# New duration estimates and a charge for array-mode changes in the list scheduler of a hybrid attention / RWKV-7 / SwiGLU block

## Chip, core and metric

The kernel runs on one core of a Trainium2 chip. The metric is device time in microseconds (us) of one execution; lower is better. Engines are named as the profile names them: PE (TensorE matmul), PEld (TensorE weight load), DVE (VectorE), ACT (ScalarE), POOL (GpSimd), SP (SyncE, which issues the DMAs).

## What is computed

One encoder block on x of 1024 x 1024 float32:

```python
h = rms_norm(x, norm_mix_pre);  proj = h @ w_in
# attention, 8 heads of 64: for query block i, over keys s < t
z = q @ k.T * 64**-0.5
log_fail = where(strict, log_sigmoid(-z), 0)
after = cumsum(log_fail, reverse=True) - log_fail        # stick breaking
o_sb = where(strict, exp(log_sigmoid(z) + after), 0) @ v
# RWKV-7, 8 heads of 64, a scan over 1024 positions
state = state * w_t + (state @ -kk_t) (kk_t * a_t)' + v_t k_t';  y_t = state @ r_t
merged = gates[:D] * (o_sb @ w_sb_out) + gates[D:] * (o_rw @ w_rw_out)
x = x + rms_norm(merged @ w_o, norm_mix_post);  h = rms_norm(x, norm_ffn_pre)
x = x + rms_norm((silu(h @ w_ffn_gate) * (h @ w_ffn_up)) @ w_ffn_down, norm_ffn_post)
```

## The kernel before

The program is written as plain Python that *records* operations (`Block.record`), and a list scheduler (`Block.schedule`) then orders them for each engine; `Block.issue` emits that order, so every instruction carries one line, L528, and the tiles' names tell them apart. All engines run their own order strictly in sequence and wait for each other by semaphores.

**What sets the order.** `cost` (line 112) gives each recorded operation an estimated duration in ns. `LATENCY` and `MARGIN` give the time from the end of one operation to the earliest start of a dependent one on another engine. `schedule` (line 381) keeps, per engine, a time from which it is free, a heap of operations that are ready by then and a heap of those that become ready later. It always advances the engine that can act first and takes the ready operation with the lowest priority number: position in the program, plus offsets (`filler()` adds 10 million, the RWKV chain subtracts 1000, the triangular inverse 300). So filler products fill an engine only while, by the estimates, nothing urgent is ready. `run` (line 448) fixes start and end; on TensorE it adds the part of a weight load that the last product doesn't cover. `choose` (line 479) prefers, after a TensorE operation estimated under 70 ns, another one under 70 ns. `grant` and `Places` hand out SBUF and PSUM buffers in the same pass, so a changed order also changes which buffer a tile gets. PSUM has 8 banks in four classes of two: d, e, c, y. Operations recorded under `together()` form a bundle: TensorE issues its products one after another with nothing between.

**Wide products.** Most TensorE work is float32 split into a high and a low float32r part: every projection is three products per 128 contraction rows (`mm3`), each with 128 x 128 weights and 512 columns. These are called wides below; in the first half of the kernel they write PSUM class d and read `big_h`.

**Stages.** About 0 to 100 us: input norm, transposes, LoRA. About 100 to 550 us: RWKV, four pairs of heads, two halves of 512 positions each, so 8 units. For each unit `rw_elementwise` prepares the operands, `rw_inverse` inverts unit triangular 32 x 32 blocks on DVE (31 rounds of a TENSOR_TENSOR with a strided operand, tiles `q<-b_nl,q`, and a TENSOR_REDUCE) followed by bundles of 32 x 32 and 64 x 64 products, and `rw_chain` (line 985) walks 8 chunks of 64 positions in sequence. One step of the chain: TensorE `px` (c<-sv,nx), then DVE copies one half of px to `xv` and ACT the other, then TensorE `ps` (c<-xv,bkt), then two DVE SCALAR_TENSOR_TENSOR write the next state `sv`. The projections of the next pair and the gate projections are the filler. About 550 to 800 us: attention, `head` (line 1124), 4 pairs of heads, per pair a stretch of 68.2 us with the same order in the first three. Per query block: score products z (PSUM class e; the masked diagonal gets a 128 x 128 bfloat16 product), ACT sigmoid to `nb`, a DVE TENSOR_TENSOR_SCAN along up to 1024 keys in place in `nb`, TensorE transposes of `nb` into PSUM class c, ACT and DVE split these into `wt` (high, low), and TensorE multiplies by v into class y. About 800 to 960 us: merge of the two branches and output projection. From about 960 us: FFN with a seven-product Strassen-like scheme.

**Array modes.** A float32 product with 64 or 32 contraction rows or output columns uses only a part of the 128 x 128 array. Such narrow products (bundles in `rw_elementwise`, `rw_inverse` and `rw_chain`) stand between full-array products.

Of the kernel before, what the change touches and what calls it, by code (L numbers as in the profile page):

```python
# [7 lines left out]
F32R = mybir.dt.float32r  # L8
# [7 lines left out]
P = 128  # L16
# [16 lines left out]
CH = 64  # L33
# [41 lines left out]
def is_ap(x):  # L75
    return hasattr(x, "tensor") and hasattr(x, "offset") and hasattr(x, "ap")


def count(shape):
    n = 1  # L80
    for d in shape:
        n *= d
    return n
# [25 lines left out]
    return [(key, p0, p1, f, f + span) for f in starts]  # L109


def cost(engine, method, kw, in_psum):

    out = kw.get("out", kw.get("ap"))
    if out is None:
        return 1283.0
    n = count(out.shape[1:])
    if engine == "tensor":
        if method == "transpose":
            return max(out.shape[0], n) / 1.2  # L120
        m, full = count(kw["lhsT"].shape[1:]), kw["lhsT"].dtype == F32
        if out.shape[0] <= CH and n <= CH:
            return 65.0 if out.shape[0] == CH else 20.0
        return 2 * max(m, n) / 1.2 if full else max(m / 1.2, n / 2.4)
    psum = any(is_ap(v) and k not in OUTS and in_psum(v) for k, v in kw.items())
    if engine == "vector":
        if method == "tensor_copy" and not psum:
            return 60 + 0.52 * n
        if method == "tensor_reduce":
            n = count(kw["in_"].shape[1:])  # L130
            return 64 + 1.042 * n
        if method == "scalar_tensor_tensor":
            return max(196, 68 + (1.16 if psum else 1.1) * n)
        return 68 + 1.042 * n
    if engine == "scalar":
        extra = "accum_out" in kw or any(is_ap(kw.get(k)) for k in ("scale", "bias"))
        return 55 + 0.833 * n + (0 if psum else 40) + (90 if extra else 0)
    if engine == "gpsimd":
        if method == "memset":
            return 40.0  # L140
        if method == "tensor_copy":
            return 120 + 3.4 * n
        if method == "tensor_scalar":
            return 320 + 2.4 * n
        return 150 + 2.1 * n
    size = 4 * count(out.shape)
    return max(450.0, size / 360.0)
# [79 lines left out]
def wait(e, to):  # L227
    return LATENCY[e][to] + (MARGIN if e != to else 0)


class Block:
# [54 lines left out]
    def in_psum(self, ap):  # L286
        return not str(ap.space).endswith("DRAM") and self.tiles[ap.offset // TSTRIDE - 1].cls.psum

    def record(self, engine, method, kw):
# [3 lines left out]
        op.prio = op.seq + self.offset  # L293
        op.steady = self.steady
        op.cost = cost(engine, method, kw, self.in_psum)
        op.preds, op.succs = set(), []
        op.bundle = self.bundle if engine == "tensor" else None
# [150 lines left out]
    def run(self, op, e, at, last, free, done, release, advance):  # L448

        if e == "tensor":  # L450
            load = count(op.kw["lhsT" if op.method == "matmul" else "in_"].shape[1:]) / 1.2
            at += max(3.0, load - last.cost if last else 0.0)
            last = op
        op.start = at
        op.end = at + op.cost
        free[e] = op.end
        done.append(op)
        for q in op.succs:
            q.ready = max(q.ready, op.end + wait(e, q.engine))
            q.left -= 1  # L460
            q.need -= 1
            if not q.left:
                release(q)
            elif not q.need:
                advance(q)
        for tile in op.tiles:
            tile.left -= 1
            tile.ends[e] = max(tile.ends.get(e, 0.0), op.end)
            if not tile.left:
                cls = tile.cls  # L470
                i, h, small = tile.where
                for k in [h] if small else [0, 1]:
                    cls.used[i][k] = None
                    cls.ends[i][k] = tile.ends if small else dict(tile.ends)
                for q in self.grant(cls):
                    release(q)
        return op.end, last
# [1098 lines left out]
```

## Time and profile before

| | |
|---|---|
| median of 3 runs | 1660.45 us (1658.56 to 1661.47) |
| profiled execution | 1659.71 us, of which the span is 1657.9 us |
| instructions | 23575 |
| PE busy | 97% of the span |
| DVE, ACT, POOL busy | 68%, 43%, 12% |
| chain that ended last | PE 74%, DVE 17%, ACT 4% |

How to read it: the span runs from the first to the last instruction, and the execution's own time lies 1.8 us above it. Records of matmuls are longer than the distance between their starts, since they are pipelined: a wide's record lasts 0.39 us or more while the next wide starts 0.23 us later. So a busy PE may still be waiting, and a wait shows as idle only beyond the tail of the record before it. Where work per stage is counted below, it is counted by distances between starts.

### The profile page before, as it was taken

The page shows a single profiled execution, that of the slowest core. Times are in us where ns is not written, and L with a number is a line of the kernel's source. Part 1 is how long each engine was busy: PE and PEld are TensorE (multiplying, and loading weights), DVE is VectorE, ACT ScalarE, POOL GpSimd, SP SyncE. Part 2 cuts the span into 40 slices and gives each one's busy share as a digit, 9 for nine tenths or more (in the row PEclk, how much of TensorE's full clock was granted, in tenths as well). Part 3 has the DMA queues.
Part 4 walks back from the last instruction along what each step waited for, and adds up shares of the span by engine and source line. Part 5 has one row for each costly group of instructions (what it writes and reads, how often), then busy time and mean ns, then how long its engine had stood idle before and what let it go on. Part 6 is the DMA issues. An engine that isn't in the chain of part 4 may idle for free.

```text
span 1657.9 us, 23575 instructions
## 1 busy us (share of the span) xinstructions
PE 1603.0 (97%) x8876; PEld 1273.8 (77%) x8876; DVE 1124.1 (68%) x1999; ACT 718.0 (43%) x1403; POOL 206.6 (12%) x344
## 2 busy tenths in 40 slices
PE   6999999999999999999999999999999999999998
PEld 5777776776777777777787788888888888888886
DVE  6567789668784877878248446766666666778484
ACT  7532334433334656566433434333233322455352
POOL 2021232512313010000015120000000000000000
PEclk9999999999999999999999999999999999999999
DMA  6533222242320000001644501233332332774455
GB/s 217 201 88 91 78 80 79 75 137 72 99 77 34 32 26 14 26 26 39 214 135 142 195 39 58 89 96 106 110 107 97 127 95 96 276 270 141 137 167 178
DMA packets 107108, 180.96 MB, mean 109 GB/s; under 512 B 42353, under 2 KB 43505, under 8 KB 106993
## 3 DMA queue, kind: packets, MB, share of 16 engines
q1 hardware_dynamic: 106992, 179.44, 33.1%
q8 instruction: 70, 1.15, 0.3%
q14 instruction: 46, 0.37, 0.1%
HBM read 129.86 MB, written 47.45 MB: 107 GB/s over the span
## 4 chain that ended last, share of the span: by engine, by line
PE 74%; DVE 17%; ACT 4%; issue 3%; DMA 2%; POOL 0%; SPq 0%; DVEq 0%; ACTq 0%; POOLq 0%
PE d_d L528 31%; PE e_e L528 17%; PE c_c L528 15%; PE y_y L528 10%; DVE q_q L528 6%; DVE b_nb L528 3%; ACT b_qst L528 1%; DVE b_wt L528 1%; DVE wlo_wlo L528 1%; DVE b_sv L528 1%; ACT whi_whi L528 1%; DVE b_nx L528 1%; ACT b_wt L528 1%; DVE b_kst L528 1%; DMA b_b<-rows 0%
## 5 line engine op out<-in xcount | busy, mean ns | idle before, releaser
L528 PE MATMUL d_d<-big_h,whi_whi 128*128 128x512 f32 x1280 | 431.5, 408 | 3.7 <-DVE b_kst L528 2.8
L528 PEld LDWEIGHTS d_d<-big_h,whi_whi 128*128 128x128 f32 x1280 | 234.7, 189 | 52.0 <-issue 6.3
L528 PE MATMUL d_d<-big_h,wlo_wlo 128*128 128x512 f32 x640 | 260.3, 407 | 0.0
L528 PEld LDWEIGHTS d_d<-big_h,wlo_wlo 128*128 128x128 f32 x640 | 120.7, 189 | 24.0 <-issue 1.9
L528 DVE TENSOR_TENSOR wlo_wlo<-raw_raw,whi_whi 128x1024 fp32r<-128x1024 f32 (+1 forms) x60 | 70.6, 1177 | 40.0 <-ACT whi_whi L528 38.6
L528 ACT CAST whi_whi<-raw_raw 128x1024 fp32r<-128x1024 f32 (+1 forms) x60 | 55.9, 933 | 92.5 <-PE d_d L528 82.5
L528 DVE TENSOR_TENSOR q_q<-b_nl,q_q 128x2 f32<-128x2 f32 (+30 forms) x248 | 85.6, 345 | 11.0 <-PE y_y L528 2.7
L528 DVE TENSOR_TENSOR_SCAN b_nb<-b_nb 128x128 f32<-128x128 f32 (+3 forms) x64 | 87.5, 1395 | 1.0
L528 POOL TENSOR_SCALAR sp_sp<-b_sv,pl_pl 64x64 f32<-64x64 f32 x120 | 58.1, 485 | 117.7 <-DVE b_sv L528 110.8
L528 DVE TENSOR_REDUCE q_q<-q_q 128x1 f32<-128x2 f32 (+30 forms) x248 | 62.1, 250 | 6.7
L528 PE MATMUL d_d<-b_wd,big_act 128*128 128x512 f32 x264 | 66.6, 395 | 0.0
L528 PE MATMUL e_e<-b_wd,big_act 128*128 128x512 f32 x264 | 66.6, 394 | 0.0
L528 ACT CAST b_wd<-b_wraw 128x512 fp32r<-128x512 f32 x71 | 42.2, 620 | 53.2 <-DVE b_wraw L528 22.7
L528 DVE TENSOR_TENSOR b_wd<-b_wraw,b_wd 128x512 fp32r<-128x512 f32 x71 | 46.7, 686 | 23.4 <-ACT b_wd L528 23.4
L528 PEld LDWEIGHTS d_d<-b_wd,big_act 128*128 128x128 f32 x264 | 49.6, 188 | 11.8
L528 PEld LDWEIGHTS e_e<-b_wd,big_act 128*128 128x128 f32 x264 | 49.6, 188 | 11.8
L528 PE MATMUL c_c<-cst_cst,b_nb 128*128 128x128 f32 x288 | 47.9, 280 | 9.2 <-DVE b_wt L528 4.5
L528 ACT COPY b_xv<-c_c 64x64 f32<-64x64 f32 x64 | 13.3, 208 | 92.1 <-DVE b_xv L528 46.6
L528 ACT CAST b_wt<-c_c 128x512 fp32r<-128x512 f32 (+2 forms) x96 | 43.9, 481 | 21.0 <-PE c_c L528 19.9
L528 DVE TENSOR_TENSOR b_wt<-c_c,b_wt 128x512 fp32r<-128x512 f32 (+2 forms) x96 | 50.0, 547 | 4.5 <-ACT b_wt L528 3.8
L528 PEld LDWEIGHTS c_c<-cst_cst,b_nb 128*128 128x128 f32 x288 | 32.6, 140 | 23.9 <-DVE b_wt L528 12.2
L528 PE MATMUL c_c<-b_wd,big_act 128*128 128x512 f32 x198 | 50.6, 395 | 0.0
(651 smaller groups left out, 3558.0 us busy)
## 6 DMA issues: line engine op xcount, KB each, us to landing
raw_raw<-w_in SPq DMA_DIRECT2D x42, 512.0 KB, 3.4
raw_raw<-w_fg SPq DMA_DIRECT2D x22, 512.0 KB, 3.5
raw_raw<-w_fu SPq DMA_DIRECT2D x22, 512.0 KB, 4.0
b_wraw<-w_fd SPq DMA_DIRECT2D x22, 512.0 KB, 5.0
act<-b_u SPq DMA_DIRECT2D x40, 256.0 KB, 3.4
b_x<-x SPq DMA_DIRECT2D x16, 512.0 KB, 6.3
raw_araw<-act SPq DMA_DIRECT2D x14, 512.0 KB, 4.3
whi_araw<-act SPq DMA_DIRECT2D x14, 512.0 KB, 4.9
```

Source lines behind the costliest of these rows:

```text
L528: getattr(getattr(self.real, op.engine), op.method)(**kw)
```

## The change

The estimates in `cost` are replaced for transposes, full float32 products, float32r products, DVE scans and DVE products whose first operand has a long element stride. A function `array_mode` tells which part of the array a TensorE operation uses, and `run` adds 90 ns when the mode changes to a partial one and 200 ns when it changes to the full one, in place of the uncovered weight load. Recorded operations, priorities, latencies and pools stay as they were.

```diff
+def array_mode(op):
+    if op.method == "transpose":
+        k, m, whole = op.kw["in_"].shape[0], P, True
+    else:
+        k, m = op.kw["lhsT"].shape[0], count(op.kw["lhsT"].shape[1:])
+        whole = op.kw["lhsT"].dtype == F32R
+    up = lambda x: 32 if x <= 32 else CH if x <= CH else P
+    return up(k), P if whole else up(m)
+INTO_PART, INTO_WHOLE = 90.0, 200.0
 def cost(engine, method, kw, in_psum):
...
         if method == "transpose":
-            return max(out.shape[0], n) / 1.2
+            return 2 + max(out.shape[0], n) / 1.2
...
-        return 2 * max(m, n) / 1.2 if full else max(m / 1.2, n / 2.4)
+        return 2 * (2 + max(m, n) / 1.2) if full else max(m / 2.4, 4.5 + 0.4435 * n)
...
+        if method == "tensor_tensor_scan":
+            return 60 + 2.083 * n
+        if method == "tensor_tensor" and abs(kw["in0"].ap[-1][0]) > 16:
+            return 68 + 1.8 * n
         return 68 + 1.042 * n
...
             load = count(op.kw["lhsT" if op.method == "matmul" else "in_"].shape[1:]) / 1.2
-            at += max(3.0, load - last.cost if last else 0.0)
+            mode = array_mode(op)
+            if last is not None and mode != array_mode(last):
+                at += INTO_WHOLE if mode == (P, P) else INTO_PART
+            else:
+                at += max(3.0, load - last.cost if last else 0.0)
```

What it moves: about half of the 7800 TensorE operations change their place, nearly all of them before the FFN. Two places show how. In the names, the letter and number ahead of the first underscore are the buffer, and the number after the name counts the tiles as they were recorded (c_825 is the same tile in both kernels); the last number counts instructions.

TensorE, in the last RWKV pair, one step of the chain: `px` is the product into c_825, `ps` the one into c_827, the products into d are wides. Before:

```order
L528 MATMUL c1_c_825_5025<-b23_sv_720_3990,b17_nx_714_4093 128x128
L528 MATMUL d1_d_888_4947<-big1_h_20_186,wlo0_wlo_883_4914 128x512
L528 MATMUL d1_d_888_4947<-big1_h_20_186,whi0_whi_882_4885 128x512
L528 MATMUL d1_d_888_4947<-big3_h_22_195,whi0_whi_882_4885 128x512
L528 MATMUL d1_d_888_4947<-big1_h_20_186,wlo0_wlo_883_4914 128x512
L528 MATMUL c0_c_827_5034<-b9_xv_722_4090,b20_bkt_723_4155 128x128
```

Now:

```order
L551 MATMUL c1_c_825_4936<-b5_sv_720_3976,b26_nx_714_4047 128x128
L551 MATMUL d0_d_879_4852<-big1_h_20_186,wlo1_wlo_876_4759 128x512
L551 MATMUL d1_d_814_4825<-big0_h_19_169,whi0_whi_810_4614 128x512
L551 MATMUL d1_d_814_4825<-big2_h_21_175,whi0_whi_810_4614 128x512
L551 MATMUL c0_c_827_4946<-b12_xv_722_3998,b15_bkt_723_4099 128x128
```

Three wides stand between the two steps of the chain instead of four, and they belong to an earlier tile of the filler: less filler has been used up by then.

DVE, in the first attention pair, where it scans the strips nb_953 and nb_958 (printed as SCALAR_TENSOR_TENSOR with one tile on both sides) between the low halves `wt` of earlier strips and the outputs `q`, `osb1` of a finished head. Before:

```order
L528 TENSOR_TENSOR b19_wt_935_5666<-c0_c_940_5642,b0_wt_933_5654 128x4x128
L528 TENSOR_TENSOR q1_q_932_5677<-q1_q_932_5677,y0_y_931_5647 64x256
L528 TENSOR_TENSOR b9_wt_936_5695<-c1_c_941_5669,b14_wt_934_5683 128x128
L528 SCALAR_TENSOR_TENSOR b10_nb_953_5660<-b10_nb_953_5660 128x896
L528 TENSOR_TENSOR b1_osb1_905_5602<-q1_q_932_5677,b11_osb0_904_5594 64x256
L528 TENSOR_TENSOR b19_wt_935_5666<-c0_c_945_5685,b0_wt_933_5654 128x4x128
L528 TENSOR_TENSOR b9_wt_936_5695<-c1_c_946_5702,b14_wt_934_5683 128x2x128
L528 SCALAR_TENSOR_TENSOR b2_nb_958_5693<-b2_nb_958_5693 128x1024
```

Now:

```order
L551 TENSOR_TENSOR b14_wt_935_5680<-c1_c_940_5659,b22_wt_933_5668 128x4x128
L551 SCALAR_TENSOR_TENSOR b17_nb_953_5653<-b17_nb_953_5653 128x896
L551 TENSOR_TENSOR q1_q_932_5700<-q1_q_932_5700,y1_y_931_5657 64x256
L551 TENSOR_TENSOR b1_wt_936_5715<-c0_c_941_5691,b7_wt_934_5706 128x128
L551 TENSOR_TENSOR b14_wt_935_5680<-c1_c_945_5697,b22_wt_933_5668 128x4x128
L551 TENSOR_TENSOR b16_osb1_905_5553<-q1_q_932_5700,b20_osb0_904_5545 64x256
L551 SCALAR_TENSOR_TENSOR b21_nb_958_5673<-b21_nb_958_5673 128x1024
L551 TENSOR_TENSOR b1_wt_936_5715<-c0_c_946_5722,b7_wt_934_5706 128x2x128
```

The scan of nb_953 stands two operations earlier, and that of nb_958 now stands ahead of the last split of the strip before it.

## Rows read from the trace of the kernel before

**Rows 1.** The page's first part: busy time, share of the span and instructions of each engine.

```profile
PE 1603.0 (97%) x8876; PEld 1273.8 (77%) x8876; DVE 1124.1 (68%) x1999; ACT 718.0 (43%) x1403; POOL 206.6 (12%) x344
```

**Rows 2.** Busy time by stage (windows in us from the span's start): length of the window, busy time of each engine with its instructions, granted TensorE clock (1.00 is 2.4 GHz), DMA share, GB/s.

```profile
100.00:550.00 450.00, 433.06 (x3445) 331.27 (x3443) 336.37 (x896) 179.68 (x385) 130.91 (x255) 1.00 0.29 82
550.00:800.00 250.00, 236.46 (x1370) 187.68 (x1369) 188.85 (x258) 153.37 (x340) 13.35 (x22) 1.00 0.10 32
800.00:960.00 160.00, 157.14 (x688) 126.40 (x687) 77.20 (x95) 66.43 (x122) 36.54 (x20) 1.00 0.49 165
960.00:1657.90 697.90, 691.42 (x3002) 559.83 (x3000) 467.29 (x687) 257.46 (x449) 9.61 (x4) 1.00 0.39 130
```

**Rows 3.** PE's instructions from 550 to 800 us grouped by tiles and shape: count, then busy us, mean ns of one record, and idle time before them with what ended it.

```profile
L528 PE MATMUL d_d<-big_h,whi_whi 128*128 128x512 f32 x338 | 111.9, 401 | 0.0
L528 PE MATMUL d_d<-big_h,wlo_wlo 128*128 128x512 f32 x168 | 68.8, 410 | 0.0
L528 PE MATMUL c_c<-cst_cst,b_nb 128*128 128x128 f32 x285 | 47.3, 280 | 8.3 <-DVE b_wt L528 4.5 <-DVE b_nb L528 2.8
L528 PE MATMUL y_y<-b_wt,b_vhl 128*64 128x256 f32 x127 | 31.3, 280 | 0.0
L528 PE MATMUL y_y<-b_wt,b_vhl 128*128 128x256 f32 x127 | 31.3, 280 | 0.0
L528 PE MATMUL e_e<-b_kst,b_ql 128*128 128x512 f32 x46 | 19.8, 431 | 0.0
L528 PE MATMUL e_e<-b_kst,b_qst 128*128 128x512 f32 x46 | 19.1, 415 | 0.0
```

**Rows 4.** PE's timeline (start us, length us, instruction, count): the first and the last row of a run of 28 wides, then four transposes and, one wide later, the next wide.

```profile
211.08 0.63 PE L528 MATMUL d_d<-big_h,whi_whi 128*128 128x512 f32 x2
...
217.57 0.40 PE L528 MATMUL d_d<-big_h,whi_whi 128*128 128x512 f32 x1
...
602.12 0.60 PE L528 MATMUL c_c<-cst_cst,b_nb 128*128 128x128 f32 x4
...
602.79 0.40 PE L528 MATMUL d_d<-big_h,wlo_wlo 128*128 128x512 f32 x1
```

**Rows 5.** PE's timeline around a bundle of 16 narrow float32 products (32 records).

```profile
223.80 0.39 PE L528 MATMUL d_d<-big_h,wlo_wlo 128*128 128x512 f32 x1
224.12 0.69 PE L528 MATMUL y_y<-q_q,q_q 32*32 32x32 f32 x32
224.75 0.73 PE L528 MATMUL d_d<-big_h,whi_whi 128*128 128x512 f32 x2
225.31 0.40 PE L528 MATMUL d_d<-big_h,wlo_wlo 128*128 128x512 f32 x1
```

**Rows 6.** Lines by shape over the whole span: the longest DVE scan and one round of the inverse, count, busy us, mean ns.

```profile
L528 DVE TENSOR_TENSOR_SCAN b_nb<-b_nb 128x1024 f32<-128x1024 f32 x8 | 18.2, 2271 | 0.0
L528 DVE TENSOR_TENSOR q_q<-b_nl,q_q 128x144 f32<-128x144 f32 x8 | 3.4, 431 | 0.2
```

**Rows 7.** Timeline of the four PE waits in one attention pair (576 to 644.2 us); in brackets the idle time before and what ended it.

```profile
585.54 1.21 PE L528 MATMUL c_c<-cst_cst,b_nb 128*128 128x128 f32 x6 [0.33 <-DVE b_wt L528]
598.51 0.66 PE L528 MATMUL c_c<-cst_cst,b_nb 128*128 128x128 f32 x4 [0.80 <-DVE b_nb L528]
620.79 0.66 PE L528 MATMUL c_c<-cst_cst,b_nb 128*128 128x128 f32 x4 [0.48 <-DVE b_wt L528]
634.69 0.33 PE L528 MATMUL y_y<-b_wt,b_vhl 128*128 128x128 f32 x1 [0.61 <-ACT b_wt L528]
```

**Rows 8.** The same pair's window, columns as in rows 2.

```profile
576.00:644.20 68.20, 64.71 (x371) 50.86 (x370) 50.30 (x70) 41.20 (x91) 5.08 (x8) 1.00 0.07 24
```

**Rows 9.** Timeline of the chain step of the first order piece: PE's px and ps, then the DVE and the ACT copy to xv.

```profile
494.89 0.38 PE L528 MATMUL c_c<-b_sv,b_nx 128*128 128x128 f32 x2
...
496.04 0.39 PE L528 MATMUL c_c<-b_xv,b_bkt 128*128 128x128 f32 x2
...
495.31 0.22 DVE L528 COPY b_xv<-c_c 64x64 f32<-64x64 f32 x1 [0.72 <-PE c_c L528]
...
495.56 0.21 ACT L528 COPY b_xv<-c_c 64x64 f32<-64x64 f32 x1 [2.33 <-DVE b_xv L528]
```

**Rows 10.** Timeline of a chain step that shares DVE with an inverse: PE, then DVE.

```profile
399.59 0.49 PE L528 MATMUL c_c<-b_sv,b_nx 128*128 128x128 f32 x2
...
401.80 0.49 PE L528 MATMUL c_c<-b_xv,b_bkt 128*128 128x128 f32 x2 [0.78 <-DVE b_xv L528]
...
401.53 0.22 DVE L528 COPY b_xv<-c_c 64x64 f32<-64x64 f32 x1
```

**Rows 11.** Waits from 100 to 550 us: engine and tile, what it waited for, us in total, times, longest us. DVE's two longest, then PE's for the chain.

```profile
DVE b_xv L528 <- PE c_c L528: 18.4, 18, 3.2
DVE b_sv L528 <- PE c_c L528: 16.9, 19, 1.4
...
PE c_c L528 <- DVE b_xv L528: 2.0, 5, 0.8
PE c_c L528 <- ACT b_xv L528: 1.5, 4, 0.5
```

**Rows 12.** PE's waits from 800 to 960 us, columns as in rows 11.

```profile
PE e_e L528 <- ACT b_woh L528: 1.3, 2, 1.1
PE d_d L528 <- DVE b_g L528: 0.8, 1, 0.8
```

## Prediction

> **What bounds the kernel.** I read the page first: PE is busy for 1603 us [rows 1]. Then busy time by stage [rows 2]. From 960 us on PE lacks 6.5 us of 697.9, most of it after the last product, and the order there moves by less than one place on average: nothing to win or lose. The idle time that an order can change lies in RWKV (16.9 us of 450) and in attention (13.5 us of 250). TensorE runs at its 2.4 GHz level in all these stages, so clock is no term.
>
> Busy time hides waits, because a record runs on after the next product has started. So I price products by distances between starts [rows 4]: 28 wides in 217.57 - 211.08 = 6.49 us, 0.232 each; four transposes and a wide in 602.79 - 602.12 = 0.67, so (0.67 - 0.232) / 4 = 0.11 per transpose. Attention then holds 338 + 168 + 46 + 46 = 598 wides or products as wide, 138.7 us, 285 transposes, 31.2, and 254 products of half the width at 0.118 (estimated by width), 30.0 [rows 3]; the 233 smaller ones of the same view, priced by width in the same way, come to 20.4. Sum 220.3: PE waits about **29.7 us of the 250**, twice what shows as idle. That is the pool from which attention can gain.
>
> **The change part by part.** *The estimates.* Each moves towards its row. Wide: 213 to 232 ns, row 232. The 1024-long scan: 1135 to 2193, row 2271 [rows 6]. One round of the inverse with 144 elements: 218 to 327, row 431 [rows 6]. A bundle in and out: entering the partial mode costs 224.12 - 223.80 - 0.232 = 0.09 us, and from 224.12 the 16 narrow products and the two wides take 1.19 where 16 x 0.032 + 0.464 = 0.98 would do (0.032 estimated from the starts inside such a bundle), so leaving costs 0.21 [rows 5]; charged are 90 and 200 ns. The charge itself saves nearly nothing, as bundles already keep narrow products together: in the order, changes into a partial mode stay at 78 and those into the full one go from 58 to 55. 3 x 0.21 = **-0.6 us**.
>
> Masks in bfloat16 and 128-wide score products fall below 70 ns in the table and are now drawn together by `choose`. They are the same products beside the same wides, and cost nothing while a wide stands on either side; were that cover gone, each draw would delay an urgent product by one short one, 0.06 us. On SP's queue no transfer moves by more than 21 places, and POOL's by 23; in attention the DMA engines are 10% busy [rows 2], so I cost that at nothing. If a weight came late, the filler's wides would be what waits.
>
> *Attention.* In one pair four waits make up 2.22 us of the 3.49 that PE is idle [rows 7, 8]. I counted in the two orders, at the prices above, what stands between the product that starts each wait's chain and the one that waits. The two waits that end on a DVE split (585.54 and 620.79) are for a PSUM buffer of class c, which DVE frees late because a scan is in front of the split. Between the two users of that buffer stood 3.0 and 2.0 us of products, and now stand 3.7 and 2.7: both waits (0.33 and 0.48) should go. The wait for the scan at 598.51 gets 3.82 in place of 3.46 us of cover, 0.36 less of its 0.80. The one before the products with v (634.69) loses 0.23 of cover. Net 0.33 + 0.48 + 0.36 - 0.23 = 0.94 of 3.49, or 27%. The same share of 29.7 is **-8.0 us**. Ends: 0, if DVE merely frees everything later, and -20, if two thirds of the pool go, as the counts say for most strips: of 96 first transposes 33 have less cover than the trace's chain needs, and 15 will. I stay near the listed waits, because the strips that open each pair (2 of 24) keep their lack. What is late next is that opening, where the scans stand behind the split of the queries.
>
> *RWKV.* The wide is now thought longer, so fewer go under each wait: 16 of the 60 chain steps have three wides between px and ps where 2 had, and between the first px and the last stand 866 wides instead of 930. These 64 x 0.232 = 14.8 us of filler run after the chain instead of inside it. Two rows price that from both sides. In a free step ACT's copy ends at 495.56 + 0.21 = 495.77, and the fourth wide starts at 496.04 - 0.23 = 495.81 [rows 9]: it covers nothing, so taking it out costs 0 to 0.05. In a step that shares DVE with an inverse the copy starts 1.94 us after px instead of 0.42, and PE idles 0.78 [rows 10]: there each wide less costs its whole 0.23. Over the stage DVE waits 18.4 + 16.9 = 35.3 us for the chain's products, PE only 3.5 for the copies [rows 11], so the chain is paced by PE more often than by DVE, and the price lies near the free end. Ends: +14.8, if all 64 were needed, and -8, half of the idle 16.9, if knowing the inverse's real length lets the scheduler place the chain's copies better. I take **+2**.
>
> By the Trainium skill ("TensorE: Matmul & The Clock Gate", section "Wait — 56ns, not 53.3ns?") products of 512 columns start 215.7 ns apart at the full clock, so the old table would be the right one. By that the 64 wides would be missing cover, 64 x 0.2157 = 13.8 us, and the sum would read +6.2. The starts 0.232 apart at clock 1.00 speak for the new table, and the measurement decides.
>
> *Output projection.* The same thinning: the transposes for the FFN's input get 2 to 6 wides less in front of them. The trace shows no wait there; the nearest ones are 1.3 and 0.8 us [rows 12]. Between 0 and +2, I take **+1**.
>
> *Sum.* -0.6 - 8.0 + 2 + 1 = -5.6 on the profiled execution's 1659.7, so 1654.1. The median of the three runs is 0.7 above that execution: **1655**.
>
> **The rivals.** *The chain loses its cover (slower).* Mechanism: the xv copies wait behind inverse rounds on DVE, ps stands three wides after px, and PE stops. RWKV +14.8; attention gains 3; with the other terms +12.2, so 1673. It decides once more than 34 of the 64 wides were needed (34 x 0.232 = 8, the gain of attention). For it: the step in rows 10, and DVE is 75% busy in this stage [rows 2]. Against: DVE waits ten times as long for PE as PE does for the copies.
>
> *The waits only move (no change).* A strip that no longer waits lets the next reach the same DVE queue sooner, and attention keeps its pace: -2, with the rest +0.4, so 1661. For it: DVE paces most of the waits listed. Against: DVE is busy for 50.3 of a pair's 68.2 us [rows 8], so it has room.
>
> *Both stages gain.* The counts hold for most strips (-16) and the chain's copies are better placed (-8): -24.6 and 1636. For it: 33 strips to 15. Against: the buffers of class c and the inverse's chain of DVE rounds stay as they were.
>
> *The old table was right.* The rule above, 1667: three wides would cover 0.65 where the copies need 0.7. The trace's 0.232 leaves it 2 in 100.
>
> **How the numbers follow.** Forecast 0.45, cover lost 0.20, waits move 0.18, both gain 0.15, old table 0.02. A measurement of this kernel tells differences from about 0.2%, 3.3 us. The forecast's own spread (attention 0 to -20, RWKV around +2) is taken as 0.33 faster, 0.11 within, 0.01 slower; both gain is faster; waits move is 0.04, 0.12, 0.02; the other two are slower. So faster 0.52, within 0.23, slower 0.25. The ends of the terms would span 1632 to 1677. For 8 in 10 the range cuts the outer half of the two extreme cases: 1638 to 1671.
>
> **What would show it.** Right: in the changed profile PE's idle time between 550 and 800 us falls by 3 to 4 us, with the waits of c on b_wt below 2 us (4.5 before); in RWKV the waits on b_xv stay below 6 us; the chain's last px comes some 10 us earlier, and a run of wides without a wait follows it. Wrong: PE's waits on b_xv and b_sv grow to 10 us or more (cover lost), or attention's waits keep their sum under other names (waits move). A span from 960 us on that differs by more than 2 us would refute the reading that the FFN is untouched.

## The result: 0.2% slower, with attention faster and RWKV slower than forecast

The changed kernel takes 1663.8 us (median of 16 runs, 1660.7 to 1668.4), the kernel before 1660.2 (16 runs, 1657.5 to 1661.8): ratio 1.0023, 95% interval 1.0015 to 1.0030. The forecast was 1655. The profiled execution of the changed kernel, 1660.73 us with a span of 1658.9, is from the low end of its runs; its trace differs by 1.0 us of span from that of before, so the signs of the stages below count more than their sum.

The page's first part after the change, as [rows 1], and the windows by stage, as [rows 2]:

```profile
PE 1603.4 (97%) x8876; PEld 1275.8 (77%) x8876; DVE 1125.2 (68%) x1999; ACT 719.2 (43%) x1403; POOL 211.2 (13%) x344
```

```profile
100.00:550.00 450.00, 424.77 (x3379) 320.22 (x3378) 331.85 (x885) 172.96 (x372) 136.15 (x253) 1.00 0.28 80
550.00:800.00 250.00, 246.10 (x1450) 201.33 (x1449) 194.18 (x269) 161.38 (x355) 14.85 (x24) 1.00 0.11 37
800.00:960.00 160.00, 154.33 (x671) 124.54 (x670) 78.80 (x95) 65.61 (x120) 32.86 (x20) 0.99 0.49 163
960.00:1658.90 698.90, 692.47 (x3007) 560.55 (x3005) 466.12 (x687) 258.59 (x449) 10.04 (x5) 1.00 0.38 130
```

PE's idle time against [rows 2]: RWKV 25.2 us (16.9 before), attention 3.9 (13.5), 800 to 960 us 5.7 (2.9), FFN 6.4 (6.5). In attention the transposes that waited 8.3 us [rows 3] now wait 0.8, and the wait of c on b_wt is gone:

```profile
L551 PE MATMUL c_c<-cst_cst,b_nb 128*128 128x128 f32 x287 | 44.6, 274 | 0.8 <-DVE b_nb L551 0.8
```

In RWKV the chain's waits have come in their place. PE's waits from 100 to 550 us (columns as in rows 11), where [rows 11] had 2.0 and 1.5 for b_xv; the first line is from the kernel before, the others from the changed one:

```profile
PE c_c L528 <- DVE b_sv L528: 0.6, 1, 0.6
...
PE c_c L551 <- DVE b_sv L551: 7.0, 8, 1.5
PE y_y L551 <- DVE q_q L551: 3.8, 3, 1.4
PE c_c L551 <- DVE b_xv L551: 3.5, 8, 1.1
PE e_e L551 <- DVE b_nx L551: 3.1, 2, 2.2
PE c_c L551 <- ACT b_xv L551: 2.6, 8, 0.9
```

And from 800 to 960 us, beside [rows 12]:

```profile
PE e_e L551 <- ACT b_woh L551: 2.3, 2, 1.8
PE y_y L551 <- DVE b_x L551: 1.8, 1, 1.8
```

Since an idle time hides the tail of the record before it, I also count waits start to start: each TensorE instruction's distance from the one before it, less the usual distance of that pair of kinds, where over 0.06 us remain. The stages here are bounded by events (first and last px of the chain, first transpose and last product with v in attention, last transpose for the FFN), so the sums hold for the work and not for a window. A product that runs at the lower clock is counted as waiting too. The differences in "all" agree with those of the profiled spans to 5 us (changed less before: 5.7 against 1.0). Sums in us, for the kernels that the argument rests on (what lies between the stages is in "all" alone):

| | before chain | chain | attention | merge, output | all |
|---|---|---|---|---|---|
| before | 15.2 | 27.5 | 23.3 | 3.9 | 69.9 |
| changed | 19.0 | 40.1 | 7.0 | 8.2 | 75.6 |
| e2 DVE's estimates alone | 14.0 | 23.0 | 2.6 | 2.6 | 42.4 |
| e3 TensorE's alone | 22.9 | 55.1 | 26.1 | 9.9 | 115.9 |
| e4 cover for px, ps | 18.5 | 41.0 | 7.0 | 7.6 | 74.5 |
| e6 changed, DVE x 1.12 | 15.5 | 20.9 | 4.8 | 7.3 | 48.5 |
| e9 the same, no charge | 15.7 | 17.4 | 5.2 | 6.9 | 45.2 |
| f1 changed, inverse cut | 19.8 | 25.6 | 6.8 | 10.5 | 63.8 |
| f2 before, inverse cut | 13.7 | 12.8 | 23.1 | 4.1 | 53.8 |

What such a chain step looks like: from the timeline of the changed kernel, one step of the last pair, DVE, POOL and PE (a few rows between left out).

```profile
511.71 1.39 DVE L551 TENSOR_TENSOR b_kst<-d_d,b_kst 64x512 fp32r<-64x512 f32 x2
511.82 0.46 PE L551 MATMUL c_c<-b_sv,b_nx 128*128 128x128 f32 x2
513.13 0.22 DVE L551 COPY b_xv<-c_c 64x64 f32<-64x64 f32 x1
513.38 2.66 DVE L551 TENSOR_TENSOR wlo_wlo<-raw_raw,whi_whi 128x1024 fp32r<-128x1024 f32 x1
...
513.64 0.49 PE L551 MATMUL c_c<-b_xv,b_bkt 128*128 128x128 f32 x2
513.67 1.28 POOL L551 TENSOR_TENSOR b_ptmp<-b_ptmp,b_v 128x512 f32<-128x512 f32 x1
...
515.96 0.27 DVE L551 SCALAR_TENSOR_TENSOR b_sv<-c_c,pl_pl,sp_sp 64x64 f32<-64x64 f32 x1
516.39 0.29 DVE L551 SCALAR_TENSOR_TENSOR b_sv<-c_c,pl_pl,sp_sp 64x64 f32<-64x64 f32 x1 [0.16 <-POOL sp_sp L551]
516.82 0.46 PE L551 MATMUL c_c<-b_sv,b_nx 128*128 128x128 f32 x2 [1.29 <-DVE b_sv L551]
```

ps has been issued at 513.64, but DVE is in a weight split that it took up at 513.38 and that the table puts at 1.13 us; it lasts 2.66. The state b_sv is late by that, and so is the next px. The chain's DVE operation isn't short of one wide of cover here; it stands behind DVE work that is longer than the scheduler thinks.

In this step the table's row is not what is wrong: the mean of such splits is 1.16 us, and this one overlaps a POOL product (see the last section). PE idles for 13.3 us ahead of px and ps between the first and the last px; 5.8 us of it, in six waits, come within 3.5 us after a DVE operation stretched in this way (before: 0.8 of 4.2 us, in two). So a part of the loss has a second cause beside the estimates, and no run separates the two. It is not what orders the runs: such stretches sum to 5.5 us inside the chain before, 9.6 changed, 4.9 in e4 and 7.5 in e2, where the chain waits 27.5, 40.1, 41.0 and 23.0 us.

### The profile page after: what moved, and what is told of

It reads as the page before. It is cut to its first block, busy times and chain, and to the rows that moved or that the text cites. A ratio compares the mean times of both kernels' runs of the same rounds, so it can differ in the third digit from the quotient of the medians.

```text
span 1658.9 us, 23561 instructions
## 1 busy us (share of the span) xinstructions
PE 1603.4 (97%) x8876; PEld 1275.8 (77%) x8876; DVE 1125.2 (68%) x1999; ACT 719.2 (43%) x1403; POOL 211.2 (13%) x344
## 4 chain that ended last, share of the span: by engine, by line
PE 73%; DVE 16%; ACT 4%; issue 3%; DMA 3%; POOL 1%; SPq 1%; DVEq 0%; POOLq 0%; ACTq 0%
PE d_d L551 31%; PE e_e L551 17%; PE c_c L551 15%; PE y_y L551 9%; DVE q_q L551 7%; DVE b_nb L551 2%; DVE b_sv L551 1%; DVE wlo_wlo L551 1%; DMA raw_raw<-w_o 1%; DVE b_bk L551 1%; DVE b_nx L551 1%; ACT whi_whi L551 1%; ACT b_qst L551 1%; SPq L551 1%; DVE b_xv L551 0%
## 5 line engine op out<-in xcount | busy, mean ns | idle before, releaser
L551 POOL TENSOR_SCALAR sp_sp<-b_sv,pl_pl 64x64 f32<-64x64 f32 x120 | 62.5, 521 | 130.0 <-DVE b_sv L551 124.3
L551 ACT COPY b_xv<-c_c 64x64 f32<-64x64 f32 x64 | 13.3, 207 | 103.1 <-PE c_c L551 59.9
L551 ACT CAST b_wt<-c_c 128x512 fp32r<-128x512 f32 (+2 forms) x96 | 44.1, 480 | 17.9 <-PE c_c L551 16.4
L551 PE MATMUL y_y<-b_wd,big_act 128*128 128x512 f32 x198 | 50.8, 395 | 0.0
L551 ACT ACTIVATE b_nb<-e_e 128x512 f32<-128x512 f32 (+2 forms) x96 | 44.7, 495 | 8.8 <-PE e_e L551 7.3
```

Of the source, the lines that this page charges most:

```text
L551: getattr(getattr(self.real, op.engine), op.method)(**kw)
```

## Experiments

Two theories at first. *Cover*: the wide is thought longer, fewer go under px and ps, and those are missing (my rival). *DVE*: the new estimate of the inverse moved the chain's DVE operations. A third, *mode*: the charge moves the bundles. The first four runs were made to tell these apart. Every run is also given by the ratio of the sums of estimates, TensorE's over DVE's; as measured it is 1554 (distances between starts, waits taken off) over 1124 (busy), 1.383. The sums leave out what `run` adds ahead of each TensorE operation (3 ns or the uncovered load), 24 to 32 us in all, while the measured 1554 contains such gaps. With it, TensorE's sum is 1475 before, in e2 and in e11 (ratios 1.566, 1.473 and 1.389), 1600 in the changed kernel (1.598) and 1585 in e9 (1.413).

| run | TensorE est. | DVE est. | ratio | us (runs) | to before, 95% |
|---|---|---|---|---|---|
| before | 1448 | 942 | 1.538 | 1659 | |
| changed | 1571 with the charge | 1001 | 1.57 | 1663.8 (16) | 1.0015 to 1.0030 |
| e1 | 1450 + 18 | 1001 | 1.467 | 1645.1 (6) | 0.9894 to 0.9932 |
| e2 | 1448 | 1001 | 1.446 | 1628.1 (4) | 0.9794 to 0.9821 |
| e3 | 1571 | 942 | 1.67 | 1706.4 (4) | 1.0266 to 1.0296 |
| e4 | 1571 | 1001 | 1.57 | 1665.6 (12) | 1.0027 to 1.0047 |
| e5 | 1553 | 1001 | 1.551 | 1654.6 (10) | 0.9959 to 0.9978 |
| e6 | 1571 | 1122 | 1.40 | 1635.9 (4) | 0.9846 to 0.9875 |
| e7 | 1553 | 942 | 1.649 | 1700.6 (4) | 1.0236 to 1.0270 |
| e8 | 1448 | 1122 | 1.291 | 1664.9 (4) | 1.0027 to 1.0057 |
| e9 | 1553 | 1122 | 1.385 | 1632.6 (5) | 0.9827 to 0.9852 |
| e10 | 1571 | 1001 | 1.57 | 1662.8 (12) | 1.0012 to 1.0031 |
| e11 | 1448 | 1062 | 1.364 | 1648.0 (5) | 0.9918 to 0.9942 |
| e12 | 1574 | 1001 | 1.57 | 1665.8 (5) | 1.0027 to 1.0051 |

**e1, the wide's old estimate.**

```diff
-        ... else max(m / 2.4, 4.5 + 0.4435 * n)
+        ... else max(m / 1.2, n / 2.4)
```

> The changed kernel with one estimate set back, that of float32r products (max(m/1.2, n/2.4)); scan, inverse, transposes and mode charge stay. In its order px and ps have 376 wides between them over the 60 chain steps (342 before the change, 317 with it). Cover theory (the longer wide takes filler out from under the chain's waits, and this costs the 11 us that RWKV lost): RWKV's waits come back from 47 to about 37 us, attention keeps its gain, 1651 us (1647 to 1656). DVE theory (the new estimate of the inverse's rounds puts the chain's DVE operations in worse places): RWKV stays at 47, 1664. Mode theory (the charge moves the bundles into the chain's way): 1664.

1645.1, 19 us below the changed kernel and lower than cover foresaw. The chain's waits fall only from 40.1 to 34.2; the rest comes from the stages before it (-4.2), attention (-3.7) and the output (-4.9). The wide's estimate acts everywhere, not in the chain above all.

**e2, DVE's two estimates alone.** The diff's scan and inverse lines on the kernel before, nothing else.

> The kernel before the change with only the two DVE estimates changed (scan and inverse round); no change on TensorE's side. Cover theory: the attention gain of 14 us comes from DVE's estimates and RWKV loses nothing, 1648 us (1644 to 1653). DVE theory: RWKV still loses its 11 us, 1660. Mode theory: 1648.

1628.1, the best of all: 31 us below before, 36 below the whole change. Every theory's figure (1648 to 1660) was too high. Windows of e2:

```profile
100.00:550.00 450.00, 436.91 (x3481) 338.78 (x3480) 340.75 (x897) 181.36 (x389) 133.62 (x255) 1.00 0.28 82
550.00:800.00 250.00, 247.89 (x1452) 206.02 (x1452) 191.13 (x265) 163.34 (x360) 14.84 (x22) 1.00 0.18 60
800.00:960.00 160.00, 159.15 (x711) 129.00 (x710) 86.97 (x106) 65.24 (x131) 40.85 (x22) 1.00 0.38 131
```

PE is idle for 13.1, 2.1 and 0.9 us: fewer than before in all three. The DVE theory falls, since these estimates help RWKV too.

**e3, TensorE's estimates and the charge alone.** The diff without its scan and inverse lines.

> The changed kernel without its two DVE estimates: only TensorE's new estimates and the mode charge. 306 wides between px and ps. Cover theory: RWKV loses its 11 us, attention gains nothing, the output stage loses 3.7: 1675 us (1669 to 1680). DVE theory: RWKV loses nothing, 1664. Mode theory: 1675.

1706.4, 47 us above before and 31 above what cover foresaw. Windows of e3:

```profile
100.00:550.00 450.00, 411.80 (x3290) 310.08 (x3290) 325.88 (x878) 166.87 (x359) 131.05 (x249) 0.98 0.27 78
550.00:800.00 250.00, 235.14 (x1323) 184.37 (x1322) 177.74 (x245) 148.34 (x326) 18.41 (x29) 1.00 0.07 24
```

PE is idle for 38.2 us in RWKV and 14.9 in attention. So the change is two halves of opposite sign: -31 by DVE's estimates, +47 by TensorE's and the charge, and together +4; the halves don't add up (+16), so each also changes what the other is worth. A part of e3's time is the clock: its 0.98 over 450 us is some 18 us at the lower level.

**e4, one wide more of cover for px and ps.** `extra` is 230 for these two products in `rw_chain` and 0 for all others.

```diff
-            q.ready = max(q.ready, op.end + wait(e, q.engine))
+            q.ready = max(q.ready, op.end + wait(e, q.engine) + (q.extra if e != "tensor" else 0.0))
...
+        b.extra = 230.0
```

> The changed kernel with all its estimates, and 230 ns (one wide) more between a DVE or ACT operation and the px or ps that waits for it, in the estimate alone: 346 wides between px and ps, 271 between ps and the next px (317 and 201 with the change). Cover theory: PE's waits on b_sv and b_xv (10.5 and 2.6 us by the profile) fall below 4 us together and RWKV wins 8 to 11 us, 1654 us (1651 to 1658). DVE theory and mode theory: the waits move with the chain, 1664; a chain that PE paces gets longer by up to 60 x 2 x 0.23 us, of which the filler then hides all.

1665.6. The waits of px and ps fall from 22.5 to 15.4 us start to start, but the chain's sum stays (40.1 and 41.0): the output products y, which wait for the inverse's q, go from 4.0 to 8.1, and the filler's products from 12.7 to 14.9. Cover as a constant per operation falls. Counting the two orders of the change in the same way (steps that pass to the other half of a pair left out) says so too: between ps and the next px stood 204 wides before and 201 now, and yet it is px whose waits grew most (from 2.2 to 10.8 us start to start).

With that I formed the ratio theory, also called pace: what counts is how fast DVE's queue runs in the estimate beside TensorE's. If DVE's work is thought too short, the scheduler puts too much of it ahead of each operation that TensorE will wait for. The first six times lie in the order of the ratios.

**e5, no charge for modes.**

```diff
-            if last is not None and mode != array_mode(last):
-                at += INTO_WHOLE if mode == (P, P) else INTO_PART
-            else:
-                at += max(3.0, load - last.cost if last else 0.0)
+            at += max(3.0, load - last.cost if last else 0.0)
```

> The changed kernel without the charge for mode changes; its estimates stay. Sum of the estimates: TensorE 1553 us, DVE 1001, ratio 1.551 (with the charge counted 1.571). Ratio theory, formed after the first four runs (what counts is how long TensorE's work is estimated against DVE's: 1.446 gave 1628, 1.467 1645, 1.538 1659, 1.571 1664, 1.669 1706, so about 350 us for a unit): 1658 us (1653 to 1663). Charge theory (of the 35.6 us between the DVE estimates alone and the whole change, the 17 between e2 and e1 are the charge's own, as it puts bundles in the chain's way): 1647 (1643 to 1651).

1654.6, inside the ratio theory's range: the charge costs 9 us, not 17, though by [rows 5] it is about what a change of mode takes.

**e6, every DVE estimate x 1.12, on the changed kernel.** `op.cost *= 1.12` for the vector engine in `record`.

> The changed kernel with every DVE estimate multiplied by 1.12, so that DVE's sum is 1122 us, about its measured busy time of 1124; ratio with the charge 1.40. Ratio theory: RWKV, attention and output all lose waits, 1625 us or less (1610 to 1635), with TensorE's new estimates and the charge in place. Charge theory: the charge's 17 us and the wide's 19 stay, since DVE's estimates were at fault only in scan and inverse: 1660 (1655 to 1666).

1635.9, 28 us below the changed kernel; 0.9 above the range, and 19 below what the charge theory allows. Its windows:

```profile
100.00:550.00 450.00, 439.45 (x3493) 339.11 (x3492) 345.58 (x904) 185.73 (x400) 137.56 (x255) 1.00 0.28 81
550.00:800.00 250.00, 246.95 (x1432) 202.36 (x1431) 187.48 (x256) 159.09 (x348) 14.25 (x22) 1.00 0.18 56
```

With TensorE's estimates and the charge all in place, PE's idle time in RWKV goes from 25.2 to 10.6 us.

**e7, every TensorE estimate x 1.0725, on the kernel before.** The same line for the tensor engine.

> The kernel before the change with every TensorE estimate multiplied by 1.0725 and nothing else: TensorE's sum is 1553 us as with the change, but no row of it is set to its own measured value and no mode is charged; DVE 942, ratio 1.649. Ratio theory: slower by about 35 to 45 us, 1695 to 1705. Charge theory: only what a longer wide costs, about 19 us, 1678 (1670 to 1685).

1700.6, as the ratio theory said: one factor, no mode, no new row, and it costs 41 us, nearly as much as e3.

**e8, e2 with every DVE estimate x 1.12.**

> The kernel of e2 (only the two DVE estimates changed, 1628 us) with every DVE estimate multiplied by 1.12: TensorE 1448 us, DVE 1122, ratio 1.29. Ratio theory: further down, 1610 to 1622 us, no lower, since e2's products find only 42 us of waits (start to start) to lose, 15 of them ahead of the chain and out of DVE's reach. Charge theory: no charge is in either, so as e2, 1628 (1623 to 1633), or slower, if DVE's operations are issued too late.

1664.9: the ratio theory missed by 43 us; in the charge theory's text the "or slower, if DVE's operations are issued too late" came true. Too long an estimate costs as well, and the scheduler's own plan shows where. In that plan (the start and end that `run` fixes) TensorE waits 17 to 21 us over the whole kernel in all the others here, 45 in e11 and 76 in e8: DVE is thought so slow that the filler is used up under it. The longest wait of e8 that isn't at the kernel's start was planned as 14.5 us and lasts 9.67. From 259.51 to 296.52 us no wide starts that writes class d. PE's timeline, what DVE waits for there, and the windows:

```profile
270.58 1.13 PE L550 MATMUL e_e<-b_tmp,cst_cst 128*128 128x512 f32 x2 [0.66 <-ACT b_tmp L550]
281.38 1.07 PE L550 MATMUL y_y<-q_q,b_nx 32*32 32x32 f32 x32 [9.67 <-DVE q_q L550]
...
296.52 0.80 PE L550 MATMUL d_d<-big_h,whi_whi 128*128 128x512 f32 x1
...
280.89 0.45 DVE L550 STREAM_TRANSPOSE q_q<-q_q 128x256 f32<-128x256 f32 x1 [7.06 <-DMA q_q<-td]
```

```profile
272.00:274.00 2.00, 0.00 (x0) 0.00 (x0) 1.82 (x4) 1.34 (x3) 0.81 (x2) 0.99 0.83 259
274.00:281.00 7.00, 0.00 (x0) 0.00 (x0) 0.11 (x1) 2.94 (x5) 1.10 (x5) 0.50 0.38 90
281.00:296.00 15.00, 9.51 (x138) 7.92 (x138) 8.15 (x34) 5.20 (x16) 3.64 (x7) 0.50 0.00 1
296.00:301.00 5.00, 4.86 (x15) 3.77 (x15) 3.02 (x10) 0.41 (x2) 3.32 (x6) 0.50 0.01 2
301.00:305.00 4.00, 4.00 (x48) 3.40 (x46) 3.36 (x11) 0.21 (x1) 1.39 (x2) 0.97 0.02 4
```

And such a wait costs twice, since the granted clock then stands at 0.50 for 27 us. The mean clock of e8's runs is 0.985 to 0.987, where e2's is 0.997 or 0.998: of two levels, that is about 50 us at the lower one beside 10, and at most 20 of the 37 us between e8 and e2 (an estimate from these figures). What filler there is waits too: the products d<-whi,h 16.9 us in all (8.9 in e2), once for 3.92 us, until ACT's b_sh has read the PSUM buffer that they need. Attention waits 18.9 us.

**e9, e6 without the charge.**

> The changed kernel without the charge and with every DVE estimate multiplied by 1.12: TensorE's sum 1553 us as with the change and as measured start to start (1554), DVE's 1122 as measured busy (1124), ratio 1.385. Ratio theory: e6 (1636) less what the charge cost in e5 (9), 1627 us (1622 to 1633), level with e2, though all of TensorE's new estimates are in it. A theory that TensorE's new estimates are harmful in themselves (each further from a good order, whatever DVE's are): not below 1640.

1632.6, at the upper end of the ratio theory's range. TensorE's new estimates do no harm in themselves: with DVE's sum set to what is measured, the chain's waits are the least of all full kernels (17.4).

**e10, 150 ns more on every edge from DVE or ACT into TensorE.**

```diff
-    return LATENCY[e][to] + (MARGIN if e != to else 0)
+    more = 150 if to == "tensor" and e in ("vector", "scalar") else 0
+    return LATENCY[e][to] + (MARGIN if e != to else 0) + more
```

> The changed kernel with 150 ns more, in the estimate alone, on every edge from DVE or ACT into TensorE: cover everywhere, but DVE's own pace in the estimate stays too fast (ratio 1.551). Pace theory (DVE falls behind its estimate by a share of all the work queued on it, some 11%, so that a constant per edge can't make it up): gains less than a third of e6's 28 us, 1656 to 1664. Cover theory (each operation lacks a constant cover of one wide or less): 1636 to 1645, as e6.

1662.8, as pace said. Its order has 349 wides between px and ps, more than before (342), and yet the chain waits 40.9 us. What waits is the same as in the changed kernel:

```profile
PE c_c L552 <- DVE b_sv L552: 6.8, 13, 1.7
PE y_y L552 <- DVE q_q L552: 5.6, 5, 2.9
PE c_c L552 <- DVE b_xv L552: 4.3, 6, 1.2
```

**e11, e2 with every DVE estimate x 1.06.**

> The kernel of e2 with every DVE estimate multiplied by 1.06: TensorE 1448 us, DVE 1062, ratio 1.364; between e2 (1.446, 1628 us) and e8 (1.291, 1665 us). Its order places 1610 wides ahead of the first transpose of attention, where e2 places 1533 and e8 1587 (before 1491, changed kernel 1459). Ratio theory: best near the measured ratio (1554 / 1124 = 1.383), 1630 us (1622 to 1640). Filler theory (e8 lost because filler that it spent under RWKV was missing in attention and its products then waited): 1610 is more than e8's, so 1665 or slower.

1648.0: neither theory. The best ratio lies above the measured 1.383, near e2's 1.446 where TensorE has its old table. Filler waits in e11 as in e8 (15.6 us), attention less (11.4 against 18.9). It is e8's trouble in small: the plan holds 45 us of TensorE waits, of which one of 7.9 us ahead of a filler product lasts 6.6 in the run, and the mean clock is 0.991 to 0.994. So the ratio alone doesn't tell the best table; it must also leave filler to the end.

**e12, a slope 0.2% steeper (0.4445 for 0.4435).**

> The changed kernel with the slope of a float32r product's estimate at 0.4445 ns for a column in place of 0.4435 (0.5 ns for a wide, 0.2%): an order that is reshuffled with the sums and the ratio unchanged. It shows how far the time moves by the reshuffling alone. Every theory: 1664 us; if it is further than 8 us off, differences of 10 us between the other runs prove little.

1665.8, 2 us from the changed kernel: this reshuffling moves the time little beside the 20 to 40 us of the others. It moves the stages more: PE idles for 21.9 us in RWKV (25.2 in the changed kernel), 7.6 in attention (3.9) and 7.5 from 800 to 960 us (5.7). So 2 to 4 us in one stage prove little.

**f1 and f2, real work taken off DVE, the orders kept.** In `rw_inverse`, on the changed kernel (f1) and, with the old estimate's slope of 1.042 for the first of the two, on the one before (f2):

```diff
+        full, n = n * (t + 1), (n + 1) // 2
+        x = nc.vector.tensor_tensor(out=tm[:, :n, : t + 1], ...)
+        x.cost = 68 + 1.8 * full
+        x = nc.vector.tensor_reduce(out=ts[:, :n, t], ...)
+        x.cost = 64 + 1.042 * full
```

> The changed kernel with every round of the triangular inverse done on half of its blocks (the two DVE instructions of a round process half the elements), while the scheduler is given the full round's estimate, so that the order of every engine is exactly the changed kernel's. It leaves out half of the inversion. DVE gets some 50 us of its work back in RWKV (149 us measured for the 496 instructions, 99 estimated), so there it keeps about the estimate's pace. Pace theory: the chain's waits (40.2 us start to start) lose 12 us or more, 1650 us or less. Cover theory (PE lacks filler in steps that share DVE with nothing): less than 5 us, 1659 or more.

> The same cut in the kernel before the change, with exactly its order: half of the inversion is left out, the scheduler sees the old full estimate. Pace theory: its chain waited less (27.5 us) and wins less, 4 to 10 us, 1649 to 1655; the difference of the two kernels in the chain's waits shrinks from 12.7 to 5 us or less, and f1 is level with this run or faster, since its attention keeps the 16 us it won. Cover theory: the difference in the chain stays, and f1 stays 2 to 6 us slower than this run.

f1 takes 1649.4 us (6 runs) and f2 1642.3 (4 runs), beside 1659.4 for before. The cut took less off DVE than I reckoned, since half the elements take 0.8 of the time; f1's lines:

```profile
L551 DVE TENSOR_TENSOR q_q<-b_nl,q_q 128x2 f32<-128x2 f32 (+30 forms) x248 | 69.8, 281 | 10.2 <-PE y_y L551 2.8 <-POOL b_nl L551 0.5
L551 DVE TENSOR_REDUCE q_q<-q_q 128x1 f32<-128x2 f32 (+30 forms) x248 | 50.7, 205 | 6.8
```

against the changed kernel's:

```profile
L551 DVE TENSOR_TENSOR q_q<-b_nl,q_q 128x2 f32<-128x2 f32 (+30 forms) x248 | 87.2, 352 | 10.4 <-PE y_y L551 2.8 <-POOL b_nl L551 0.8
L551 DVE TENSOR_REDUCE q_q<-q_q 128x1 f32<-128x2 f32 (+30 forms) x248 | 62.0, 250 | 6.8
```

29 us less DVE work (149.2 to 120.5) took 14.5 us off the chain's waits in the changed order, as pace said, and 14.7 in the old one, where pace said 4 to 10. So DVE's real work sets the size of these waits, with nothing changed on TensorE. But the difference between the two orders stayed, 12.8 us after 12.6, and f1 is 7 us slower than f2; my expectation that both would close was wrong, and on this point cover's statement (the difference stays) held. What makes the changed order the worse of the two is thus not shown by this pair.

**What joins them** is a count by chain step, worked out from the traces: DVE's records from one xv copy to the next (with 0.05 us allowed for each instruction's issue; in the trace the next record starts some 0.03 us after the end of one or 0.09 before it), less TensorE's starts from one px to the next without waits, summed over the steps in which DVE has more. It is 21.3 us in e9, 21.7 in f2, 28.3 in e6, 28.9 in e2, 29.5 in f1, 36.0 before, 42.8 changed, 48.0 in e10, 52.7 in e3; TensorE's waits in the 60 steps are 14.4, 9.6, 19.2, 17.9, 24.0, 20.9, 35.5, 38.1 and 48.7. The change put DVE work of longer real time beside shorter TensorE work in 38 steps (33 before). The cut of f1 and f2 lowers both kernels' excess by 13 to 14 and leaves the distance. These are nine of the sixteen kernels. A coarser recount of all sixteen, some 10 us higher throughout, puts e8 and e11 (33.6 and 35.3) next to e9 (33.0), although they take 15 to 32 us longer: what these two lose lies outside the steps of the chain, in the planned waits told under e8. This is a count that orders the chain's waits, not a separate experiment.

## Why the prediction was wrong

*Failed step: the price of the 64 wides in RWKV.* The prediction took "+2", "near the free end", between -8 and +14.8. Measured, the chain's waits rose by 12.6 us. The rival *the chain loses its cover* had the place and nearly the size (14.8; 1673 against 1663.8), and its sign came true (waits on b_xv and b_sv of 13.1 us, where 10 were named). That its size is near is luck: of the 64 wides 25 stood between px and ps and 3 between ps and the next px, the others where the chain passes from one half or pair to the next. At their whole price 28 wides are 6.5 us, and more wides didn't help in e4 and e10. The argument for the free end was that DVE waits 35.3 us for the chain's products and PE only 3.5 for the copies [rows 11], "so the chain is paced by PE more often than by DVE". That compares sums over unlike steps. In the rows DVE waits in a free step [rows 9] and PE in one that shares DVE with an inverse [rows 10], and idle time of the one kind does nothing for the other; over the 60 steps PE's waits go with the excess of DVE work (the count above). And I looked at b_xv alone; two thirds of the loss are px waiting for the state b_sv (start to start 2.2 before, 10.8 now).

*A mis-sized term: attention, -8.* It measured -16.3 start to start, inside the end of -20 that the count of strips gave; I had taken the four listed waits instead. Its cause was right: e3, without the DVE estimates, has 26.1 us of waits in attention, e2 with them alone 2.6. "c on b_wt below 2 us" came true, as it is gone, and the idle time fell by 9.6 where 3 to 4 were named.

*A mis-sized term: output, +1.* It measured +4.3, again with b_woh as the longest. Here the clock, which the prediction took for no term, has a part: after that wait it stands at 0.50 for about 3 us (last section).

*Left out: the work ahead of the chain*, +3.8. I costed nothing there. What makes these waits longer was not looked into; this and the output's are of the size by which e12's reshuffling moves a stage.

These four terms sum to +4.4 us, where the medians differ by 3.6 and the profiled spans by 1.0.

*Right:* the FFN is untouched (6.4 us of lack after 6.5), and the charge saves nothing by itself. It isn't free, though: e5 says it costs 9 us by the other orders it makes, and e9 against e6, where DVE's estimates are raised, 3 us. Against the forecast of "some 10 us earlier", the last px comes 3 us earlier (531.7 to 528.8): the waits of the chain and of the work ahead of it ate the rest.

*The old table as the right one* (the rule of the Trainium skill, "TensorE: Matmul & The Clock Gate", section "Wait — 56ns, not 53.3ns?", given 0.02): its time, 1667, is nearly what came, but its premise is refuted. In the changed kernel two wides and the next start are 902.88 - 902.42 = 0.46 us apart, so 0.23 each:

```profile
902.42 0.62 PE L551 MATMUL e_e<-b_woh,big_m 128*128 128x512 f32 x2
902.88 0.39 PE L551 MATMUL e_e<-b_wol,big_m 128*128 128x512 f32 x1
```

The new estimate is near the true one: with the 3 ns that `run` adds, a wide is put at 235 ns now and was at 216. In the same way TensorE's whole sum was 5% short before and is 3% long now (1475 and 1600 for 1554); DVE's was 16% short and is still 11% short (1001 for 1124), and in the chain 26% (215 for 290 us, by the sum of records, which overlap a little). The table before was a clock that ran fast for both. The change set TensorE's nearly right and DVE's half right, and the order that came out trusts DVE to be where it isn't. That this costs the time is shown by e6, which sets DVE's sum right and wins 28 us, and by e7, which lengthens TensorE's alone and loses 41.

*Open:* why e2 beats e9, whose estimates are nearer to what is measured for both; what in the changed order keeps the chain's waits 12.8 us above those of the order before when DVE has less work (f1, f2); and how much of them the stretched DVE operations make.

## What to carry over

In a list scheduler the estimates of two engines act against each other: correcting one side alone can lose more than the old, equally wrong table, so move the estimates of the engine that paces the waits first (e2: -31 us), and test each side by itself before both. Look at the waits in the plan as well: where they grow, as in e8 and e11, the filler runs out. A cover of filler is to be judged in the steps where the other engine has more work than the bottleneck, by real durations, not by sums of waits over a stage. Here the version to keep is e2, the two DVE estimates alone, at 1628.1 us, 0.979 to 0.982 of the kernel before.

## What the runs showed of the hardware

*A POOL product can hold up DVE.* In the chain step shown above, the split of a weight takes 2.66 us while POOL runs a TENSOR_TENSOR of 1.28 us; the mean of that group is 1.163:

```profile
L551 DVE TENSOR_TENSOR wlo_wlo<-raw_raw,whi_whi 128x1024 fp32r<-128x1024 f32 (+1 forms) x60 | 69.7, 1163 | 57.9 <-ACT whi_whi L551 53.1 <-PE d_d L551 4.8
```

Of the DVE instructions that last over 0.15 us longer than the median of their shape, nearly all overlap a POOL TENSOR_TENSOR (26 of 27 before, 30 of 31 now), and the stretch sums to 21.6 us before and 25.8 now over the span. No estimate knows of it. By the Trainium skill ("SBUF — State Buffer", section "SBUF: two separate sides") the two share a port pair that one holds for its whole instruction, against DVE operations with two SBUF inputs too; the trace agrees in kind: in the kernel before, of the DVE instructions that overlap such a POOL product none of 46 with an operand in PSUM is stretched, and of the TENSOR_TENSORs wholly in SBUF 20 of 42. That page of the Trainium skill says that whoever starts first has it; by the records DVE started first here, at 513.38 against 513.67, and it was still the one to be stretched.

*The clock can fall at a wait.* In e8 PE is idle from 271.7 to 281.4 us; the granted clock falls to 0.50 (the 1.2 GHz level) at about 274, and is at 1.00 again from about 301, some 5 us after wides run again. In the changed kernel PE is idle for 1.82 us up to 905.32: the window from 906 to 907 us reads 0.50, that from 909 to 910 us 1.00, and the wides at 0.50 start 906.63 - 906.20 = 0.43 us apart. After the 1.50 us up to 283.56 us in the same kernel the clock stays at 1.00.

```profile
905.32 1.08 PE L551 MATMUL e_e<-b_woh,big_m 128*128 128x512 f32 x2 [1.82 <-ACT b_woh L551]
906.20 0.63 PE L551 MATMUL e_e<-b_wol,big_m 128*128 128x512 f32 x1
906.63 1.05 PE L551 MATMUL e_e<-b_woh,big_m 128*128 128x512 f32 x2
```

```profile
283.00:285.00 2.00, 1.41 (x6) 0.93 (x7) 1.94 (x5) 0.59 (x3) 1.50 (x4) 1.00 0.00 0
...
906.00:907.00 1.00, 1.00 (x3) 0.76 (x3) 1.00 (x1) 0.00 (x0) 0.24 (x1) 0.50 1.04 414
...
909.00:910.00 1.00, 1.00 (x6) 0.79 (x6) 1.00 (x2) 0.00 (x0) 0.00 (x0) 1.00 0.97 320
```

Of the changed kernel's 16 runs the one with the lowest mean clock (0.994) is the slowest, 1668.4 us, and the five fastest stand at 0.997 or 0.998. So such drops are a part of the spread over 8 us; the eight runs at 0.998 alone spread over 3.4 us.
